# A decoder trunk of two layers: the seventh product moved between two halves of an up projection, and a weight sum made by an accumulating DMA

## The chip, the cores and the metric

The kernel runs on one NeuronCore of a Trainium2 chip. The metric is the device time of one execution in microseconds; the time before is the median of three runs. TensorE does the matmuls, VectorE (DVE), ScalarE (ACT) and GpSimd (POOL) the elementwise work, SyncE (SP) issues most of the loads from HBM. Each engine takes its own instructions in a fixed order, and an instruction that waits for a semaphore holds up all that stand behind it on its engine.

## The reference

Two post-norm layers over 512 positions of width 1024, in float32. The first has retention and stick-breaking attention heads, the second differential attention; both end in the same gated MLP, and the change lies in that MLP alone:

```
def conv_ffn(x, w_up, conv_w, conv_b, w_down):
    S = x.shape[1]
    h = x @ w_up                                   # 512 x 5632
    hp = jnp.pad(h, ((0, 0), (CONV_W - 1, 0), (0, 0)))
    h = sum(hp[:, j:j + S] * conv_w[j] for j in range(CONV_W)) + conv_b
    u, g = jnp.split(h, 2, axis=-1)                # 2 x 2816
    return (jax.nn.silu(g) * u) @ w_down           # 2816 x 1024
...
for l in range(DEPTH):
    m = mixer(x)                                   # even or odd
    x = layer_norm(ALPHA * x + m, ln1_g[l], ln1_b[l])
    f = conv_ffn(x, w_up[l], conv_w[l], conv_b[l], w_down[l])
    x = layer_norm(ALPHA * x + f, ln2_g[l], ln2_b[l])
```

## The kernel before

**Precision.** Every large product is made of three matmuls (`mm3`, L148 to L150): each operand is split into a high part (ScalarE casts it, L132: `wh`) and a low part (VectorE subtracts, L134: `wl`), and high by high, high by low and low by high are added in PSUM.

**The MLP's stages.** The 2816 columns are 22 blocks of 128. `period(i)` (L535) does block i: `up_mm` makes its two halves, first the column block of u, then that of the gate, each 24 matmuls into a PSUM bank of its own (`mmps`). `conv_half` (L445) takes a half out of PSUM: one ScalarE activation (L447) and two VectorE instructions (L449). `gated` (L454) applies silu (ScalarE, L456) and multiplies (VectorE, L457).

**The down projection by groups.** Blocks 0 to 15 form four groups of four, and the down projection of a group is done as a 2 by 2 block product with seven products m1 to m7 in place of eight. The four periods of the next group issue them (j = 0 to 3 is the period's place in its group): after the up projection m2 and m1 at j = 0, m5 at j = 1, m6 and m3 at j = 2, m7 at j = 3, and m4 of the group at j = 0 of the group after. Each product is twelve matmuls, six into each of two PSUM banks. m1, m6, m7 and m4 share the pair `wine`, m2, m5 and m3 the pair `winc`. After each product VectorE adds or subtracts the two banks into the residual `x` (`update`, L478; its instruction is L485 at the first touch of a piece of x and L482 later). A product that writes a pair again waits until VectorE has read it: m4 waits for the update after m7, and the next m1, which starts the pair anew, for the update after m4.

**The weights.** w_down of a group is stored as four blocks 21, 11, 22, 12 of 1024 columns. Three sums of blocks are made in the tile `chain`: SyncE loads 11, and GpSimd's queue adds 12, then 22, then 21 by accumulating DMAs (L476); between them the two splits read the sum. The other products read two tiles `raw` of 2048 columns (`wsrc`, L184): half 0 holds blocks 21 and 11, half 1 blocks 22 and 12. In half 1 GpSimd adds block 22 onto block 12 (L192), which is the fourth sum. `raw` has two buffers, the split weights `wh`, `wl` three. Half 1 is loaded, added and split in the `begin_to` of period j = 1 (L545).

**The order.** In the periods the order of ScalarE, VectorE and GpSimd is the order of the code, as is TensorE's everywhere. At j = 0 with g >= 1 the code issues: both up halves; `conv_half` of the first; the pending low parts of the group (`left`); the split of `chain` and the chain's next DMA; `conv_half` of the second and `gated`; then m4 of the group before with its update, m2 and m1 with theirs, and the split of the weights of block i + 2. Two layers with four groups each make eight m4 (three of the four groups of a layer have one in front of their m2 and m1; the fourth m4 stands in block 20).

Of the kernel before, what the change touches and what calls it, by code (L numbers as in the profile page):

```python
# [13 lines left out]
ALU = mybir.AluOpType  # L14
# [5 lines left out]
S = 512  # L20
# [6 lines left out]
ALPHA = (2 * DEPTH) ** 0.25  # L27
# [6 lines left out]
UNIT = 1024  # L34
# [80 lines left out]
class Build:  # L115
# [64 lines left out]
    def prefetch(self, ahead):  # L180
        while self.csrc and sum(c.n for c in self.cget.values()) < ahead * UNIT:
            self.begin()

    def wsrc(self, key):  # L184
        nc = self.nc
        if key[0] == "quad":
            _, l, g, half = key
            raw = self.load(self.a["w_quad"][l][g][:, half * 2 * UNIT:(half + 1) * 2 * UNIT])
            c = self.weights(self.wp)
            if half:  # L190
                self.split(raw, c, 0)
                nc.gpsimd.tensor_tensor(raw[:, UNIT:], raw[:, UNIT:], raw[:, :UNIT], op=ALU.add)  # L192
                return self.split(raw, c, UNIT)
            return self.split(raw, c, 0, UNIT)
        if key[0] == "tail":
            _, l, i = key
            raw = self.load(self.a["w_down"][l][i])
            return Pair(*(self.split(raw[:, a:a + UNIT], self.weights(self.w2, UNIT), 0) for a in (0, UNIT)))
        src = self.a[key[0]]
        for i in key[1:]:  # L200
            src = src[i]
        raw = self.load(src)
        return self.split(raw, self.weights(self.wp), 0, UNIT)
# [155 lines left out]
    def setup(self, ctx):  # L359
        nc = self.nc  # L360
        P_ = lambda name, bufs=1, **kw: ctx.enter_context(self.pool(name, bufs, **kw))
        self.ctx = ctx
        self.constp = P_("const")
        self.smallp = P_("small", 3)
        self.xtp = P_("xt")
        self.rawp = P_("raw", 2)
        self.wp = P_("w", 3)
        self.actp = P_("act", 16)
        self.mmps1 = P_("mmps", 3, space=PSUM)
        self.trps = P_("trps", 2, space=PSUM)  # L370
        self.dramp = P_("dram", 1, space=DRAM)
        self.mmi = 0
        self.mmpools = [(self.mmps1, "mm")]
        self.x = P_("xn", 1, side="right").tile([P, TB, DM], F32, tag="x", name="x")
        self.new_xT()
        self.ident = self.constp.tile([P, P], F32, tag="ident", name="ident")
        make_identity(nc, self.ident)
        self.mhalf = self.constp.tile([P, 8], F32, tag="mhalf", name="mhalf")
        nc.vector.memset(self.mhalf, -0.5)
        self.one = self.constp.tile([P, 1], F32, tag="one", name="one")  # L380
        nc.vector.memset(self.one, 1.0)
# [15 lines left out]
    def ffn(self, l, ln1):  # L397
        nc = self.nc
        with ExitStack() as c2:
# [44 lines left out]
            def conv_half(i, f, ps):  # L444
                tag, n = ("cu", 3) if f == i else ("cg", 2)  # L445
                t = tp.tile([P, S], F32, tag=tag, name=self.nm("cvt"), bufs=n)
                nc.scalar.activation(t, ps, AF.Identity, bias=cv[:, f, 3:4], scale=cv[:, f, 2:3])  # L447
                for d, c in ((1, 1), (2, 0)):
                    nc.vector.scalar_tensor_tensor(  # L449
                        out=t[:, d:], in0=ps[:, :S - d], scalar=cv[:, f, c:c + 1], in1=t[:, d:],  # L450
                        op0=ALU.mult, op1=ALU.add)
                return t
# [12 lines left out]
            full = slice(0, S)  # L465
            banks, quads, touched = {}, {}, set()

            def chain(g, *blocks):

                for b in blocks:  # L470
                    src = self.a["w_quad"][l][g][:, BLOCKS.index(b) * UNIT:(BLOCKS.index(b) + 1) * UNIT]
                    if b == "11":
                        self.chain = self.chainp.tile([P, UNIT], F32, tag="chain", name=self.nm("chain"))
                        nc.sync.dma_start(out=self.chain, in_=src)
                    else:
                        nc.gpsimd.dma_start(out=self.chain, in_=src, accum_op=ALU.add)  # L476

            def update(ps, tb, half, sign):  # L478
                xs = self.x[:, tb, half * S:(half + 1) * S]
                op = ALU.add if sign > 0 else ALU.subtract  # L480
                if (tb, half) in touched:
                    nc.vector.tensor_tensor(xs, xs, ps, op=op)  # L482
                else:
                    touched.add((tb, half))
                    nc.vector.scalar_tensor_tensor(out=xs, in0=xs, scalar=ALPHA, in1=ps, op0=ALU.mult, op1=op)  # L485

            def product(g, name):

                if name in ("m5", "m6", "m4"):
                    w = quads.pop((g, {"m5": "p1", "m6": "p2", "m4": "p4"}[name]))  # L490
                    at = 0
                else:
                    if name in ("m2", "m3"):
                        quads[g, name] = self.chunk(("quad", l, g, int(name == "m3")), 0)
                    w = quads[g, "m2" if name in ("m2", "m1") else "m3"]
                    at = UNIT if name in ("m1", "m7") else 0
                for tau in range(2):
                    if name == "m1":
                        banks["e", tau] = ps2.tile([P, S], F32, tag="e", name=self.nm("wine"), bufs=2)
                    elif name in ("m2", "m5"):  # L500
                        banks["c", tau] = self.trps.tile([P, S], F32, tag="tr", name=self.nm("winc"))
                    ps = banks["e" if name in ("m1", "m6", "m7", "m4") else "c", tau]
                    first = name in ("m1", "m2", "m5")
                    ts = slice(tau * P, (tau + 1) * P)
                    for kk in range(2):
                        h, l_ = ops[g, name, kk]
                        self.mm3(ps, h[:, ts], l_[:, ts], *w.get(at + kk * S, S), first and kk == 0, kk == 1,
                                 skip_group_check=not first)
                    lo, hi = tau, 2 + tau
                    tb, half, sign = {"m1": (lo, 0, -1), "m2": (lo, 0, 1), "m5": (hi, 1, 1), "m6": (lo, 1, 1),  # L510
                                      "m3": (lo, 1, 1), "m7": (hi, 1, 1), "m4": (hi, 0, -1)}[name]
                    update(ps, tb, half, sign)

            keys = []
            for i in range(NPAIR):
                keys.append(("w_up", l, i))
                g, j = i // 4 - 1, i % 4
# [5 lines left out]
            w = [self.chunk(("w_up", l, i), 4) for i in range(2)]  # L523
            pss = [[self.mmps() for _ in range(2)] for _ in range(2)]
# [10 lines left out]
            def period(i, left):  # L535
                g, j = i // 4 - 1, i % 4
                quad = 0 <= g < QUADS
                w = self.chunk(("w_up", l, i), 0)
                pss = [self.mmps(), self.mmps()]
                for k in range(2):  # L540
                    self.up_mm(w, k, pss[k], full)
                if not quad:
                    self.begin_to(("w_up", l, i + 2) if i + 2 < NPAIR else dk[2 * (i + 2 - NPAIR)])
                elif j < 3:
                    self.begin_to((("w_up", l, i + 1), ("quad", l, g, 1), ("w_up", l, i + 1))[j])  # L545
                u = conv_half(i, i, pss[0])
                if left:
                    left()
                if quad and j < 3:
                    name = ("p1", "p2", "p4")[j]  # L550
                    quads[g, name] = self.split(self.chain, self.weights(self.w2, UNIT), 0)
                    if j < 2:
                        chain(g, ("22", "21")[j])
                if j == 2 and g + 1 < QUADS:
                    chain(g + 1, "11", "12")
                left = gated(i, u, conv_half(i, NPAIR + i, pss[1]))
                if j == 0 and g >= 1:
                    product(g - 1, "m4")
                if quad:
                    for name in (("m2", "m1"), ("m5",), ("m6", "m3"), ("m7",))[j]:  # L560
                        product(g, name)
                    if j in (0, 2):
                        self.begin_to(("w_up", l, i + 2))
                return left

            E = mybir.EngineType
# [17 lines left out]
            for u in range(8):  # L584
                tb, half = u // 2, u % 2
                if u < 2:
                    ps = first[u]
                    down_mm(ps, 0, half, LASTN - 1)
                else:
                    ps = self.mmps()  # L590
# [587 lines left out]
```

## Time and profile before

| | |
|---|---|
| median of 3 runs | 1245.32 us (1243.57 to 1248.01) |
| profiled execution | 1244.74 us, of which the span is 1242.9 us |
| TensorE's granted clock, mean | 0.993 of full speed |
| busy share of the span | TensorE 97%, VectorE 70%, ScalarE 47%, GpSimd 15% |
| DMA | 140.13 MB, mean 113 GB/s |
| GpSimd's add of block 22 (L192) | 8 times, 2383 to 2677 ns, median 2401 ns |

The span runs from the first instruction to the last. Rows of the timeline give the start in us, the duration in us, engine, line, operation and tiles (out<-in), and in brackets how long the engine was idle before it and what ended that. "x2" is two instructions in a row, with the duration of both together. A matmul row shows 0.39 us because matmuls overlap in the pipeline; their starts are 0.23 us apart at full clock.

### The profile page before, as it was taken

How to read it: one execution, taken by the hardware profiler on the slowest of the kernel's cores; microseconds unless marked ns; L12 is line 12 of the kernel's file. 1: busy time of each engine (PE TensorE's matmuls, PEld its weight loads, DVE VectorE, ACT ScalarE, POOL GpSimd, SP SyncE). 2: the span in 40 equal slices, each digit the busy share in tenths (PEclk: the TensorE clock that was granted, in tenths of full speed). 3: DMA queues.
4: the chain of work that ended last, by engine and by line, in shares of the span. 5: the costliest groups of instructions: out<-in, count | busy, mean ns of one | idle time of the engine just before them, and what ended most of it. 6: DMA issues, size and time to landing. Idle time of an engine off the chain costs nothing.

```text
span 1242.9 us, 15110 instructions
## 1 busy us (share of the span) xinstructions
PE 1208.8 (97%) x5876; PEld 1001.4 (81%) x5876; DVE 869.6 (70%) x1324; ACT 581.2 (47%) x902; POOL 180.3 (15%) x238
## 2 busy tenths in 40 slices
PE   8999999999999999999999999999999999998997
PEld 6888877888887888788878888787988878787886
DVE  4866588776778677766655658776678777766664
ACT  5455565444534443433335658763444444443331
POOL 0211132211212121200000101011022211211000
PEclk9999999999999999999999999999999999998999
DMA  8322112333363535332252213223435444435111
GB/s 317 125 85 87 50 70 75 104 127 113 87 185 92 165 99 157 114 119 102 105 166 102 77 51 111 86 70 112 136 102 152 122 134 126 121 116 144 68 68 68
DMA packets 28175, 140.13 MB, mean 113 GB/s; under 512 B 3830, under 2 KB 4639, under 8 KB 15560
## 3 DMA queue, kind: packets, MB, share of 16 engines
q1 hardware_dynamic: 24648, 126.59, 28.7%
q0 software_dynamic: 3456, 12.58, 6.6%
q8 instruction: 46, 0.75, 0.3%
q14 instruction: 25, 0.20, 0.1%
HBM read 137.04 MB, written 4.74 MB: 114 GB/s over the span
## 4 chain that ended last, share of the span: by engine, by line
PE 79%; DVE 11%; ACT 5%; issue 2%; POOL 1%; DMA 1%; POOLq 0%; DVEq 0%; ACTq 0%; SPq 0%
PE mmps L148 21%; PE mmps L149 21%; PE mmps L150 21%; DVE wl L134 3%; PE wine L148 2%; PE wine L150 2%; PE wine L149 2%; DVE cvt L449 1%; PE winc L149 1%; PE winc L148 1%; PE winc L150 1%; PE dacc L939 1%; DVE cvt L457 1%; DVE actl L346 1%; PE dz L338 1%
## 5 line engine op out<-in xcount | busy, mean ns | idle before, releaser
L148 PE MATMUL mmps<-xTh,wh 128*128 128x512 f32 (+1 forms) x1008 | 384.8, 382 | 5.7 <-ACT wh L230 5.2
L149 PE MATMUL mmps<-xTl,wh 128*128 128x512 f32 (+1 forms) x1008 | 380.4, 377 | 0.9 <-DVE xTl L1080 0.9
L150 PE MATMUL mmps<-xTh,wl 128*128 128x512 f32 (+1 forms) x1008 | 379.8, 377 | 0.5 <-DVE wl L134 0.5
L134 DVE TENSOR_TENSOR wl<-raw,wh 128x1024 fp32r<-128x1024 f32 x196 | 240.1, 1265 | 33.0 <-ACT wh L132 32.7
L132 ACT CAST wh<-raw 128x1024 fp32r<-128x1024 f32 x196 | 195.3, 1045 | 76.9 <-PE mmps L149 35.8
L148 PEld LDWEIGHTS mmps<-xTh,wh 128*128 128x128 f32 x1008 | 190.6, 189 | 39.8 <-ACT wh L230 5.2
L150 PEld LDWEIGHTS mmps<-xTh,wl 128*128 128x128 f32 x1008 | 190.4, 189 | 36.1 <-DVE wl L134 1.0
L149 PEld LDWEIGHTS mmps<-xTl,wh 128*128 128x128 f32 x1008 | 190.6, 189 | 34.2 <-DVE xTl L1080 1.6
L449 DVE SCALAR_TENSOR_TENSOR cvt<-mmps,cv,cvt 128x511 f32<-128x511 f32 (+1 forms) x176 | 130.7, 747 | 109.1 <-ACT cvt L447 106.2
L447 ACT ACTIVATE cvt<-mmps,cv 128x512 f32<-128x512 f32 x88 | 68.3, 778 | 215.3 <-PE mmps L150 215.3
L148 PE MATMUL mmps<-wh,acth 128*128 128x512 f32 x224 | 91.4, 408 | 0.1
L150 PE MATMUL mmps<-wh,actl 128*128 128x512 f32 x224 | 88.5, 395 | 0.0
L149 PE MATMUL mmps<-wl,acth 128*128 128x512 f32 x224 | 88.3, 394 | 0.0
L148 PE MATMUL mmps<-wh,xTh 128*128 128x512 f32 x160 | 64.9, 406 | 0.0
L456 ACT ACTIVATE cvt<-cvt 128x512 f32<-128x512 f32 x44 | 27.8, 632 | 77.5 <-DVE cvt L449 77.5
L457 DVE TENSOR_TENSOR cvt<-cvt,cvt 128x512 f32<-128x512 f32 x44 | 39.4, 895 | 33.4 <-ACT cvt L456 33.4
L150 PE MATMUL mmps<-wh,xTl 128*128 128x512 f32 x160 | 62.6, 391 | 0.0
L149 PE MATMUL mmps<-wl,xTh 128*128 128x512 f32 x160 | 62.5, 390 | 0.0
L476 POOL DMA_DIRECT2D chain<-in_w_quad x24 | 21.4, 890 | 235.8 <-DVE wl L134 161.9
L150 PEld LDWEIGHTS mmps<-wh,actl 128*128 128x128 f32 x224 | 42.4, 189 | 10.3 <-DVE actl L349 0.5
L148 PEld LDWEIGHTS mmps<-wh,acth 128*128 128x128 f32 x224 | 42.4, 189 | 9.7 <-DVE x L276 0.7
L149 PEld LDWEIGHTS mmps<-wl,acth 128*128 128x128 f32 x224 | 42.4, 189 | 7.8
(190 smaller groups left out, 1800.1 us busy)
## 6 DMA issues: line engine op xcount, KB each, us to landing
raw<-in_w_up SPq DMA_DIRECT2D x44, 1024.0 KB, 5.0
raw<-in_w_quad SPq DMA_DIRECT2D x16, 1024.0 KB, 4.9
chain<-in_w_quad POOLq DMA_DIRECT2D x24, 512.0 KB, 6.1
raw<-in_w_ot SPq DMA_DIRECT2D x8, 1024.0 KB, 4.8
raw<-in_w_et SPq DMA_DIRECT2D x6, 1024.0 KB, 4.8
raw<-in_w_en SPq DMA_DIRECT2D x6, 1024.0 KB, 4.9
raw<-in_w_down SPq DMA_DIRECT2D x6, 1024.0 KB, 5.0
raw<-in_w_oe SPq DMA_DIRECT2D x4, 1024.0 KB, 4.8
```

Of the source, the lines that this page charges most:

```text
L132: nc.scalar.copy(c.h[:, sl], raw[:, sl])
L134: nc.vector.tensor_tensor(c.l[:, sl], raw[:, sl], c.h[:, sl].bitcast(F32), op=ALU.subtract)
L148: mm(out, lh, rh, start=start, stop=False, **kw)
L149: mm(out, lh, rl, start=False, stop=False, **kw)
L150: mm(out, ll, rh, start=False, stop=stop, **kw)
L338: self.nc.tensor.matmul(out, lhs, B[:, 2 + m, 0:n], start=False, stop=True)
L346: nc.vector.tensor_tensor(l, src, h.bitcast(F32), op=ALU.subtract)
L447: nc.scalar.activation(t, ps, AF.Identity, bias=cv[:, f, 3:4], scale=cv[:, f, 2:3])
L449: nc.vector.scalar_tensor_tensor(out=t[:, d:], in0=ps[:, :S - d], scalar=cv[:, f, c:c + 1], in1=t[:, d:], op0=ALU.mult, op1=ALU.add)
L456: nc.scalar.activation(g, g, AF.Silu)
L457: nc.vector.tensor_tensor(u, u, g, op=ALU.mult)
L476: nc.gpsimd.dma_start(out=self.chain, in_=src, accum_op=ALU.add)
```

## The change

`product` no longer issues its own update but returns what `update` needs. In the period at j = 0 with g >= 1, m4 of the group before is issued between the two up halves, and its update after `conv_half` of the first half. And half 1 of a group's weights is loaded by `load_quad` at the end of period j = 0; block 22 is added onto block 12 there by a DMA from GpSimd's queue that reads block 22 from HBM again. The split of half 1 stays at j = 1, and casts both parts before both subtractions.

```diff
+    def load_quad(self, key):
+
+        _, l, g, half = key
+        src = self.a["w_quad"][l][g][:, half * 2 * UNIT:(half + 1) * 2 * UNIT]
+        raw = self.load(src)
+        if half:
+            self.nc.gpsimd.dma_start(out=raw[:, UNIT:], in_=src[:, :UNIT], accum_op=ALU.add)
+            self.early[key] = raw
+        return raw
+
     def wsrc(self, key):
         nc = self.nc
         if key[0] == "quad":
-            _, l, g, half = key
-            raw = self.load(self.a["w_quad"][l][g][:, half * 2 * UNIT:(half + 1) * 2 * UNIT])
-            c = self.weights(self.wp)
-            if half:
-                self.split(raw, c, 0)
-                nc.gpsimd.tensor_tensor(raw[:, UNIT:], raw[:, UNIT:], raw[:, :UNIT], op=ALU.add)
-                return self.split(raw, c, UNIT)
-            return self.split(raw, c, 0, UNIT)
+            raw = self.early.pop(key, None) or self.load_quad(key)
+            return self.split(raw, self.weights(self.wp), 0, UNIT)
...
-                for k in range(2):
-                    self.up_mm(w, k, pss[k], full)
+                self.up_mm(w, 0, pss[0], full)
+                m4 = j == 0 and g >= 1 and product(g - 1, "m4")
+                self.up_mm(w, 1, pss[1], full)
...
                 u = conv_half(i, i, pss[0])
+                if m4:
+                    update(m4)
                 if left:
                     left()
...
                 left = gated(i, u, conv_half(i, NPAIR + i, pss[1]))
-                if j == 0 and g >= 1:
-                    product(g - 1, "m4")
                 if quad:
                     for name in (("m2", "m1"), ("m5",), ("m6", "m3"), ("m7",))[j]:
-                        product(g, name)
+                        update(product(g, name))
                     if j in (0, 2):
                         self.begin_to(("w_up", l, i + 2))
+                    if j == 0:
+                        self.load_quad(("quad", l, g, 1))
                 return left
```

TensorE in the first layer's second group, before, at the end of the first up half (`mmps_3119` is the bank of the first half, `mmps_3120` that of the second, `wine_2784` the first bank of m4):

```order
L148 MATMUL mmps_3119<-xTh_2062,wh_3025 128x512
L149 MATMUL mmps_3119<-xTl_2063,wh_3025 128x512
L150 MATMUL mmps_3119<-xTh_2062,wl_3026 128x512
L148 MATMUL mmps_3120<-xTh_2062,wh_3025 128x512
L149 MATMUL mmps_3120<-xTl_2063,wh_3025 128x512
```

The same place after the change:

```order
L148 MATMUL mmps_3119<-xTh_2062,wh_3025 128x512
L149 MATMUL mmps_3119<-xTl_2063,wh_3025 128x512
L150 MATMUL mmps_3119<-xTh_2062,wl_3026 128x512
L148 MATMUL wine_2784<-wh_2982,a_357_2521 128x512
L149 MATMUL wine_2784<-wl_2983,a_357_2521 128x512
```

m4's twelve matmuls stand now in front of the 24 of the second half; before they stood behind them.

VectorE in the same period, before (`wine_2784`, `wine_2792` are m4's banks, `winc` those of m2, `wine_3238` the first of m1):

```order
L449 SCALAR_TENSOR_TENSOR cvt_3185<-mmps_3119,cv_2232,cvt_3185 128x510
L346 TENSOR_TENSOR actl_3190<-q_3091,acth_3189 128x512
L346 TENSOR_TENSOR actl_3194<-q_3091,acth_3193 128x512
L134 TENSOR_TENSOR wl_3198<-chain_2986,wh_3197 128x1024
L449 SCALAR_TENSOR_TENSOR cvt_3202<-mmps_3120,cv_2232,cvt_3202 128x511
L449 SCALAR_TENSOR_TENSOR cvt_3202<-mmps_3120,cv_2232,cvt_3202 128x510
L457 TENSOR_TENSOR cvt_3185<-cvt_3185,cvt_3202 128x512
L485 SCALAR_TENSOR_TENSOR x<-x,wine_2784 128x512
L485 SCALAR_TENSOR_TENSOR x<-x,wine_2792 128x512
L482 TENSOR_TENSOR x<-x,winc_3222 128x512
L482 TENSOR_TENSOR x<-x,winc_3230 128x512
L482 TENSOR_TENSOR x<-x,wine_3238 128x512
```

And after the change (its lines are numbered 4 or 5 higher here):

```order
L454 SCALAR_TENSOR_TENSOR cvt_3197<-mmps_3119,cv_2232,cvt_3197 128x510
L490 SCALAR_TENSOR_TENSOR x<-x,wine_2784 128x512
L490 SCALAR_TENSOR_TENSOR x<-x,wine_2791 128x512
L350 TENSOR_TENSOR actl_3204<-q_3091,acth_3203 128x512
L350 TENSOR_TENSOR actl_3208<-q_3091,acth_3207 128x512
L134 TENSOR_TENSOR wl_3212<-chain_2986,wh_3211 128x1024
L454 SCALAR_TENSOR_TENSOR cvt_3216<-mmps_3120,cv_2232,cvt_3216 128x511
L454 SCALAR_TENSOR_TENSOR cvt_3216<-mmps_3120,cv_2232,cvt_3216 128x510
L462 TENSOR_TENSOR cvt_3197<-cvt_3197,cvt_3216 128x512
L487 TENSOR_TENSOR x<-x,winc_3222 128x512
L487 TENSOR_TENSOR x<-x,winc_3229 128x512
L487 TENSOR_TENSOR x<-x,wine_3238 128x512
```

The update after m4 has moved up by six instructions; it no longer stands behind the second half's convolution and the multiplication. On GpSimd the accumulating DMA stands in the very place of the add: behind the chain's DMA of block 22, in front of that of block 21. SyncE's loads keep their order, but for one load for the second layer's mixer at the end of the first layer, which now stands behind two small ones.

## Rows read from the trace of the kernel before

**Rows 1.** the page: span; TensorE's busy us, share, instructions
```profile
span 1242.9 us, 15110 instructions
PE 1208.8 (97%) x5876; PEld 1001.4 (81%) x5876; DVE 869.6 (70%) x1324; ACT 581.2 (47%) x902; POOL 180.3 (15%) x238
```

**Rows 2.** TensorE's waits on wine banks: us in all, times, longest
```profile
PE wine L148 <- DVE x L482: 7.6, 3, 3.2
PE wine L148 <- DVE x L485: 3.2, 2, 1.7
```

**Rows 3.** timeline of TensorE: first matmuls of m2 and m4 (start, us)
```profile
328.42 0.39 PE L148 MATMUL winc<-wh,ah 128*128 128x512 f32 x1
388.51 0.39 PE L148 MATMUL wine<-wh,a 128*128 128x512 f32 x1
391.31 0.40 PE L148 MATMUL winc<-wh,ah 128*128 128x512 f32 x1
453.28 0.39 PE L148 MATMUL wine<-wh,a 128*128 128x512 f32 x1
516.55 0.39 PE L148 MATMUL wine<-wh,a 128*128 128x512 f32 x1
584.16 0.39 PE L148 MATMUL wine<-wh,a 128*128 128x512 f32 x1
989.40 0.39 PE L148 MATMUL wine<-wh,a 128*128 128x512 f32 x1
1119.04 0.39 PE L148 MATMUL wine<-wh,a 128*128 128x512 f32 x1
1188.24 0.39 PE L148 MATMUL wine<-wh,a 128*128 128x512 f32 x1
```

**Rows 4.** windows behind two waits: busy by engine, PEclk, DMA share, GB/s
```profile
525.00:530.00 5.00, 4.85 (x14) 3.88 (x15) 3.03 (x6) 0.55 (x1) 0.00 (x0) 0.66 0.00 0
1128.00:1134.00 6.00, 6.00 (x14) 4.72 (x15) 2.84 (x5) 0.93 (x2) 0.00 (x0) 0.50 0.01 3
```

**Rows 5.** timeline at the first wait: VectorE, GpSimd, TensorE
```profile
386.84 1.52 DVE L449 SCALAR_TENSOR_TENSOR cvt<-mmps,cv,cvt 128x511 f32<-128x511 f32 x2
392.15 2.39 POOL L192 TENSOR_TENSOR raw<-raw 128x1024 f32<-128x1024 f32 x1 [0.27 <-DMA raw<-in_w_quad]
392.90 2.20 DVE L457 TENSOR_TENSOR cvt<-cvt,cvt 128x512 f32<-128x512 f32 x1 [0.76 <-ACT cvt L456]
395.02 1.27 DVE L485 SCALAR_TENSOR_TENSOR x<-x,wine 128x512 f32<-128x512 f32 x2
395.84 0.47 PE L148 MATMUL wine<-wh,ah 128*128 128x512 f32 x1 [1.57 <-DVE x L485]
```

**Rows 6.** timeline, earlier there: update after m7, second up half
```profile
378.22 0.69 DVE L457 TENSOR_TENSOR cvt<-cvt,cvt 128x512 f32<-128x512 f32 x1 [0.76 <-ACT cvt L456]
380.93 1.27 DVE L482 TENSOR_TENSOR x<-x,wine 128x512 f32<-128x512 f32 x2
383.07 0.39 PE L148 MATMUL mmps<-xTh,wh 128*128 128x512 f32 x1
```

**Rows 7.** timeline there: SyncE's load, GpSimd's chain DMA, ScalarE's casts
```profile
386.95 0.33 SPq L143 DMA_DIRECT2D raw<-in_w_quad  x1
391.00 0.88 POOL L476 DMA_DIRECT2D chain<-in_w_quad  x1 [8.57 <-DVE wl L134]
398.88 2.01 ACT L132 CAST wh<-raw 128x1024 fp32r<-128x1024 f32 x2 [4.12 <-PE wine L150]
```

**Rows 8.** GpSimd's chain DMAs: landing; page part 3, their queue
```profile
DMA to landing us min/median/max: 5.7/6.1/7.7
q0 software_dynamic: 3456, 12.58, 6.6%
```

**Rows 9.** timeline, next periods: second sum's low part, and m6
```profile
406.58 1.22 DVE L134 TENSOR_TENSOR wl<-chain,wh 128x1024 fp32r<-128x1024 f32 x1
423.26 0.39 PE L148 MATMUL wine<-wh,acth 128*128 128x512 f32 x1
```

More of the change, by code (lines that the diff above doesn't have):

```diff
@@ L372, in setup @@
         self.mmi = 0
+        self.early = {}
         self.mmpools = [(self.mmps1, "mm")]
@@ L476, in chain, with update @@
                         nc.gpsimd.dma_start(out=self.chain, in_=src, accum_op=ALU.add)
[L478 to L485, printed above, removed]
+            def update(parts):
+                for ps, tb, half, op in parts:
+                    xs = self.x[:, tb, half * S:(half + 1) * S]
+                    if (tb, half) in touched:
+                        nc.vector.tensor_tensor(xs, xs, ps, op=op)
+                    else:
+                        touched.add((tb, half))
+                        nc.vector.scalar_tensor_tensor(out=xs, in0=xs, scalar=ALPHA, in1=ps, op0=ALU.mult, op1=op)
             def product(g, name):
+                res = []
                 if name in ("m5", "m6", "m4"):
@@ L509, in product @@
                     lo, hi = tau, 2 + tau
-                    tb, half, sign = {"m1": (lo, 0, -1), "m2": (lo, 0, 1), "m5": (hi, 1, 1), "m6": (lo, 1, 1),
-                                      "m3": (lo, 1, 1), "m7": (hi, 1, 1), "m4": (hi, 0, -1)}[name]
-                    update(ps, tb, half, sign)
+                    tb, half = {"m1": (lo, 0), "m2": (lo, 0), "m5": (hi, 1), "m6": (lo, 1), "m3": (lo, 1),
+                                "m7": (hi, 1), "m4": (hi, 0)}[name]
+                    res.append((ps, tb, half, ALU.subtract if name in ("m1", "m4") else ALU.add))
+                return res
             keys = []
```

## The prediction

> **What bounds the kernel now.** I read the page first. TensorE is busy for 1208.8 of the span's 1242.9 us [rows 1]; VectorE comes next with 70%. Nothing but TensorE's own idle or slow time is to be had, some 34 us of idle in all. So the second view was the list of TensorE's waits. In the MLP two entries stand out, both on the first product that needs the `wine` banks anew, both ended by VectorE's update: three waits with 7.6 us together and two with 3.2 us [rows 2]. That is m1, waiting for the update after m4: five waits, 10.8 us.
>
> The third view, TensorE's timeline, tells what those waits cost in all. From one group's m4 to the next TensorE's program is always the same (four up projections, seven products), so the distance should be constant. In the first group, which has no m4 in front of its m2, the distance from m2 to the next m2, with one m4 in it, is 391.31 - 328.42 = 62.89 us [rows 3]. The six groups that have m4 in front of m1 take 64.77, 63.27 and 67.61 us in the first layer, and 129.64 (two together) and 69.20 us in the second [rows 3], 394.49 us in all. Five of them hold the five waits; the sixth, 63.27, holds none that the list counts and bounds the undisturbed pitch from above. I take 63.0, nearer to the group that surely waits for nothing: 394.49 - 6 x 63.0 = 16.5 us are lost. With 62.89 it is 17.2, with 63.27 it is 14.9.
>
> The 16.5 us can be checked from other rows. 10.8 us are the waits. Behind the two longest waits the granted clock falls: 0.66 over 5 us and 0.50 over 6 us [rows 4], where 1.00 is 2.4 GHz and 0.50 is 1.2 GHz. That is 5 x 0.34 + 6 x 0.50 = 4.7 us. The remaining 1.0 us is the refilling of the matmul pipeline after each wait (a first matmul of 0.47 us in rows 5 against 0.39).
>
> Why is VectorE late there? In rows 5 it takes the first up half at 386.84. Then come other work, the second half, and the multiplication at 392.90, which takes 2.20 us where the same instruction takes 0.69 at 378.22 [rows 6]; it lies beside GpSimd's add of 2.39 us, which started at 392.15. Only at 395.02 does the update after m4 start, and TensorE's m1 at 395.84.
>
> **Part 1: m4 between the two halves.** The matmuls are the same. A half lasts 388.51 - 383.07 = 5.44 us, a product 391.31 - 388.51 = 2.80 us [rows 3, 6]. So in this group m4 now starts at 383.07 and ends at 385.87, the second half ends at 391.31, m2 begins there as before, and m1 could begin at 391.31 + 2.80 = 394.11; it began at 395.84, a delay of 1.73 us.
>
> m4's update now stands behind the first half's convolution on VectorE, which ends at 386.84 + 1.52 = 388.36 [rows 5]. Two instructions of 1.27 us together end at 389.63, 4.5 us ahead of m1. The wait goes, and nothing on VectorE is late in its place: what moves behind the update (1.27 us) used to stand before it, and the second half itself now ends 2.80 us later, so its convolution waits for TensorE in any case.
>
> What is late next? m4 itself: it starts one half earlier, and needs the update after m7. That runs at 380.93 for 1.27 us, so both banks are free at 382.20, 0.87 us before 383.07; the first bank, which m4 needs first, about 0.6 us earlier [rows 6]. The margin is thin but positive, and nothing in the change stands in front of that update.
>
> The second half's path (convolution, silu, product, split) comes 2.80 us later. Its next user on TensorE is a whole up projection away or further: 10.88 us (two halves) in block 20, more in the groups. Cost: 0. If that cover were gone it would cost up to 2.80 us in each of eight places.
>
> **Part 2: the fourth sum by DMA.** Eight adds of 2.4 us leave GpSimd, which is idle for 85% of the span. The VectorE instruction beside each gets back up to 2.20 - 0.69 = 1.5 us. On the path this is worth nothing beyond part 1, since the update no longer stands behind it; without part 1 it would shorten most of the waits. Added are eight DMAs of 512 KB (4.2 MB on 140) and a new wait: the second cast of half 1 on ScalarE waits for the landing.
>
> When does it land? The load of half 1 is issued at 386.95 and has landed by 392.15, where the add could start [rows 5, 7]. The chain's DMA stands ahead on GpSimd at 391.00 and moves back by the update's 1.27 us to 392.27; with its 0.88 us the new DMA is issued at 393.15. No row has an accumulating DMA onto `raw`, or two from GpSimd's queue back to back. Lower bound: it lands like the chain's, 6.1 us after issue, at 399.3. Upper bound: the two are served one after the other; the 24 DMAs of that queue took 6.6% of 1242.9 us [rows 8], 3.4 us each, so the second lands 3.4 us behind the first (392.27 + 6.1 = 398.4), at 401.8. I take 401.8, as the two are issued 0.9 us apart.
>
> Who waits? ScalarE wants the first cast at 398.88 - 1.73 = 397.15 and the second 1.0 us later, at 398.15 [rows 7]. It waits 1.1 to 3.6 us. Behind it on ScalarE and VectorE stand the convolution of the next period's first half, which TensorE finishes at 396.91 + 5.44 = 402.35, and the second weight sum's split. That split's low part was ready at 407.80, and m6, its first user, starts at 423.26: 15.5 us of slack [rows 9], against a delay of at most about 1 us. Cost: 0. Below nothing it cannot go, as no TensorE wait hangs on half 1 now.
>
> A rule of the Trainium skill speaks against this edit (SBUF — State Buffer, section "SBUF: two separate sides"): a DMA from GpSimd's queue can starve while VectorE holds the port through which its descriptors are written, in its example 620 ns became about 3100. Here the 24 such DMAs landed in 5.7 to 7.7 us with VectorE busy for 70% of the time [rows 1, 8], so no starving of that size shows; by the rule the landing would be an estimated 2.5 us later (from that page's two figures), still far from m6, and the sum would stay.
>
> **The sum.** Profiled execution 1244.74 us (span 1242.9, 1.84 around it) - 16.5 = 1228.2. The median of the runs is 0.6 us above the profiled execution, so 1228.8 us. With the pitch's bounds: 1228.1 to 1230.4.
>
> **The rivals.**
>
> *The clock is not given back.* If the two half-clock stretches are not the doing of the waits, 4.7 us stay: 1233.5. For it: rows 4 show the stretches, not their cause. Against: both lie where m1 begins in the two groups with the largest distances, 8 to 9 us behind their m4 [rows 3, 4].
>
> *m4 waits in m1's stead.* If the update after m7 slips by more than 0.87 us against TensorE, each further us costs one us in eight places. VectorE's largest slip in rows 5 is 1.5 us, beside the add that goes; at twice that, 3.0 us, the cost is 8 x 2.1 = 17 us at worst and all of the gain: 1246. A slip of 1.5 us costs 8 x 0.6 = 5: 1234. Against: the work ahead of that update is untouched.
>
> *The move does not do what it says.* m1 has other needs (its weights' low part, the operands); if one of these is due at the same moment, the wait only changes its name: 1245. Against: the weights' subtraction stands ahead of the 386.84 row on VectorE, over 7 us before m1.
>
> *The DMA lands too late: slower.* ScalarE stands still on the second cast, with all convolutions behind it. It reaches TensorE only beyond the 15.5 us of rows 9, a landing at 398.15 + 15.5 = 413.7, 20.5 us after issue. To be slower by 0.3% (3.7 us, about what a measurement of this kernel tells from no change) it must take 16.5 + 3.7 = 20.2 us in eight places, 2.5 each: 23 us from issue to landing against 7.7 at most in rows 8. Then the time is 1249 or more.
>
> **How the numbers follow.** Forecast 0.81; clock not given back 0.05; m4 waits 0.07 (two thirds of it at a small slip); wait renamed 0.04; landing too late 0.03. Faster by over 0.3%: 0.81 + 0.05 + 0.05 = 0.91; within: 0.04 + 0.01 = 0.05; slower: 0.03 + 0.01 = 0.04. The range goes from 1228.1 less the spread of the runs (1245.32 - 1243.57 = 1.75), 1226, up to the small-slip and clock cases (1234) with the same spread, 1236.
>
> **What would show it.** Right: TensorE's list has no wait on `wine` for VectorE; the distances from m4 to m4 are all 63.0 to 63.3 us; the clock is 1.00 behind every m1; the multiplication after the gate takes 0.7 us at j = 0; ScalarE shows some us of waiting for a DMA into `raw` at j = 1, and TensorE none after it. Wrong: a wait of m4 for the update after m7, in every group alike; a TensorE wait on an up half or on m6 at j = 1 or 2; or distances that stay above 64 us without a wait.

## The result

| | before | changed |
|---|---|---|
| median of the runs, us | 1244.44 (4 runs, 1242.00 to 1248.01) | 1226.70 (4 runs, 1226.15 to 1226.91) |
| profiled execution, us | 1244.74 | 1226.91 |
| its span, us | 1242.9 | 1225.1 |

The ratio is 0.9854, with a 95% interval of 0.9829 to 0.988: the change makes the kernel faster by 17.7 us. The forecast was 1228.8.

The page of the changed kernel (span; busy us, share of the span and instructions by engine; GpSimd's DMA queue with packets, MB and share), against [rows 1, 8]:

```profile
span 1225.1 us, 15125 instructions
PE 1202.3 (98%) x5876; PEld 998.8 (82%) x5876; DVE 859.0 (70%) x1324; ACT 581.1 (47%) x902; POOL 167.8 (14%) x238
q0 software_dynamic: 4608, 16.78, 8.5%
```

TensorE executes the same 5876 instructions. VectorE and GpSimd lose some 11 and 13 us of busy time, and the queue carries eight more transfers. The list of TensorE's waits (us in all, times, longest) holds no entry on `wine` any more, where [rows 2] had five waits with 10.8 us. Its longest entries now are:

```profile
PE mmps L148 <- ACT wh L234: 4.5, 1, 4.5
PE atr L710 <- ACT zp L702: 3.6, 2, 2.1
PE dz L341 <- ACT kB L333: 1.3, 2, 1.1
```

The timeline of TensorE, first matmuls of m4 in both layers (start and duration in us), against the m4 rows of [rows 3]:

```profile
382.56 0.39 PE L148 MATMUL wine<-wh,a 128*128 128x512 f32 x1
445.48 0.39 PE L148 MATMUL wine<-wh,a 128*128 128x512 f32 x1
508.39 0.39 PE L148 MATMUL wine<-wh,a 128*128 128x512 f32 x1
571.30 0.39 PE L148 MATMUL wine<-wh,a 128*128 128x512 f32 x1
976.29 0.39 PE L148 MATMUL wine<-wh,a 128*128 128x512 f32 x1
1039.20 0.39 PE L148 MATMUL wine<-wh,a 128*128 128x512 f32 x1
1102.12 0.39 PE L148 MATMUL wine<-wh,a 128*128 128x512 f32 x1
1165.03 0.39 PE L148 MATMUL wine<-wh,a 128*128 128x512 f32 x1
```

The distances from m4 to m4 are 62.91 or 62.92 us everywhere: (571.30 - 382.56) + (1165.03 - 976.29) = 377.48 us for the six groups that took 394.49 before. So 17.0 of the 17.8 us of span come from them. The rest lies outside: the first m2 starts at 327.91 us in place of 328.42 [rows 3], and from the fourth m4 to the fifth, between the layers, it takes 404.99 us in place of 405.24.

VectorE and TensorE of the changed kernel at the first m1 that has an m4 in front of it (start, duration; in brackets idle time before and its releaser), against [rows 5, 6]:

```profile
380.43 1.27 DVE L487 TENSOR_TENSOR x<-x,wine 128x512 f32<-128x512 f32 x2
386.33 1.52 DVE L454 SCALAR_TENSOR_TENSOR cvt<-mmps,cv,cvt 128x511 f32<-128x511 f32 x2
387.77 1.27 DVE L490 SCALAR_TENSOR_TENSOR x<-x,wine 128x512 f32<-128x512 f32 x2
391.83 1.53 DVE L454 SCALAR_TENSOR_TENSOR cvt<-mmps,cv,cvt 128x511 f32<-128x511 f32 x2 [0.45 <-ACT cvt L452]
393.57 0.39 PE L148 MATMUL wine<-wh,ah 128*128 128x512 f32 x1
394.13 0.69 DVE L462 TENSOR_TENSOR cvt<-cvt,cvt 128x512 f32<-128x512 f32 x1 [0.76 <-ACT cvt L461]
```

The update after m4 (387.77) ends at 389.04, 4.5 us ahead of m1 at 393.57, which waits for nothing. The multiplication takes 0.69 us in place of 2.20. The update after m7 ends at 381.70, 0.86 us ahead of m4 at 382.56.

Windows around two m1 of the changed kernel, at the places of [rows 4] (us; busy us of TensorE, its weight loads, VectorE, ScalarE and GpSimd, each with its instructions; granted clock, DMA share, GB/s):

```profile
517.00:524.00 7.00, 7.00 (x33) 5.74 (x32) 5.07 (x9) 4.58 (x6) 1.78 (x2) 1.00 0.70 117
1110.00:1120.00 10.00, 10.00 (x46) 8.24 (x45) 8.07 (x11) 5.27 (x7) 1.77 (x2) 1.00 0.66 120
```

The granted clock is 1.00 in both, where it was 0.66 and 0.50; windows of 8 us at the four other m1 behind an m4 (from 393, 456, 986 and 1049 us) read 1.00 too. Last, the new transfers and who waits for them, in three views: GpSimd's issues (ns, starts) and their landing; ScalarE's waits for them (us in all, times, longest); and ScalarE's timeline at the first:

```profile
L190 POOL DMA_DIRECT2D raw<-in_w_quad x8: 1037/1104/1189, 332.2 to 1112.0; - x8
DMA to landing us min/median/max: 7.6/8.2/9.3
```
```profile
ACT wh L132 <- DMA raw<-in_w_quad: 26.6, 8, 4.7
```
```profile
400.54 1.05 ACT L132 CAST wh<-raw 128x1024 fp32r<-128x1024 f32 x1 [2.97 <-DMA raw<-in_w_quad]
```

ScalarE stands still for 3.3 us on average in eight places (26.6 / 8), and no wait of TensorE follows from it.

### The profile page after: what moved, and what is told of

It reads as the page before. It is cut to its first block, busy times and chain, and to the rows that moved or that the text cites. A ratio compares the mean times of both kernels' runs of the same rounds, so it can differ in the third digit from the quotient of the medians.

```text
span 1225.1 us, 15125 instructions
## 1 busy us (share of the span) xinstructions
PE 1202.3 (98%) x5876; PEld 998.8 (82%) x5876; DVE 859.0 (70%) x1324; ACT 581.1 (47%) x902; POOL 167.8 (14%) x238
## 4 chain that ended last, share of the span: by engine, by line
PE 88%; DVE 5%; ACT 4%; POOL 1%; DMA 1%; issue 1%; POOLq 0%; DVEq 0%; ACTq 0%
PE mmps L148 22%; PE mmps L149 22%; PE mmps L150 22%; PE wine L149 2%; PE wine L148 2%; PE wine L150 2%; PE winc L149 2%; PE winc L148 2%; PE winc L150 2%; PE dacc L949 1%; DVE wl L134 1%; PE dz L342 1%; DVE t L698 1%; PE dz L341 1%; POOL zp L701 1%
## 5 line engine op out<-in xcount | busy, mean ns | idle before, releaser
L462 DVE TENSOR_TENSOR cvt<-cvt,cvt 128x512 f32<-128x512 f32 x44 | 30.4, 692 | 32.6 <-ACT cvt L461 32.6
L1063 ACT ACTIVATE junk<-x,lst 128x1024 bf16<-128x1024 f32 x16 | 18.4, 1150 | 64.5 <-DVE lst L1060 64.4
```

What stands on the lines that cost most here:

```text
L462: nc.vector.tensor_tensor(u, u, g, op=ALU.mult)
L1063: nc.scalar.activation(junk, x, AF.Square, bias=st[:, 0:1], accum_out=st[:, 1:2])
```

## The experiments

The theory: TensorE lost its time because m4's update stood behind the second half's multiplication in VectorE's order; the update's place is what counts, GpSimd's add made it worse, and the DMA is hidden behind slack. The rivals: the matmuls' place counts; the DMA brings part of the gain, or costs something; and m4 or half 1 could still become the late ones. Edits are against the changed kernel; the kernel before ran beside each group (medians 1243.12, 1244.71 and 1244.12).

**The move alone.** GpSimd's add is back, and half 1 is loaded, added and split at j = 1 again.

```diff
 wsrc:
-    raw = self.early.pop(key, None) or self.load_quad(key)
-    return self.split(raw, self.weights(self.wp), 0, UNIT)
+    _, l, g, half = key
+    raw = self.load(self.a["w_quad"][l][g][:, half * 2 * UNIT:(half + 1) * 2 * UNIT])
+    c = self.weights(self.wp)
+    if half:
+        self.split(raw, c, 0)
+        nc.gpsimd.tensor_tensor(raw[:, UNIT:], raw[:, UNIT:], raw[:, :UNIT], op=ALU.add)
+        return self.split(raw, c, UNIT)
+    return self.split(raw, c, 0, UNIT)
...
 period:
-    if j == 0:
-        self.load_quad(("quad", l, g, 1))
```

> m4 and its update stand as in the changed kernel; the fourth weight sum is made by GpSimd's add again, as before. Theory A (the update's place on VectorE carries the whole gain; the DMA has nothing left to save): 1226 to 1228 us, m4 to m4 distances 62.9 us, no TensorE wait on wine; the multiplication beside the add takes about 2.2 us again, and nobody waits for it. Theory B (the add's drag on VectorE is a part of the loss in its own right): 1231 us or more, with TensorE waits on wine of 0.5 us and up.

Measured: 1226.34 us (ratio 0.987, 0.9855 to 0.9885), distances of 62.91 and 62.92, no wait on `wine`. GpSimd and VectorE in its timeline:

```profile
392.29 2.70 POOL L202 TENSOR_TENSOR raw<-raw 128x1024 f32<-128x1024 f32 x1
394.12 1.43 DVE L468 TENSOR_TENSOR cvt<-cvt,cvt 128x512 f32<-128x512 f32 x1 [0.76 <-ACT cvt L467]
```

The add still slows the multiplication (1.43 us against 0.69, and not the 2.2 that were expected), and it costs nothing: once the update has moved, no one waits there. The DMA half of the change brings nothing on top.

**The DMA alone.** m4 and its update are where they were.

```diff
-m4 = j == 0 and g >= 1 and product(g - 1, "m4")
...
-if m4:
-    update(m4)
...
 left = gated(i, u, conv_half(i, NPAIR + i, pss[1]))
+if j == 0 and g >= 1:
+    update(product(g - 1, "m4"))
```

> The sum by the accumulating DMA, m4 and its update behind both up halves as before. Theory A: the multiplication takes 0.7 us in place of 2.2, so the update comes 1.5 us earlier; the waits of m1 shrink to about 0.2 us in four groups and 1.5 to 1.7 us in the last group of each layer, where a split stands ahead of the update as well, and the clock does not fall behind waits of that size; some 4.7 us of the 17 remain: 1231 us (1229 to 1234). Theory B (the DMA does nothing for TensorE): 1243 to 1246 us.

Measured: 1231.98 us (0.9916, 0.9901 to 0.9931). TensorE's waits on `wine`:

```profile
PE wine L148 <- DVE x L487: 2.9, 2, 1.5
```

Four of six distances are 63.27 or 63.28, two 64.66 and 64.67, which is 382.44 us in all. So either half takes away most of the loss, by the distances 12 us this one (394.49 - 382.44) and 17 the other: two cures for one wait.

**Matmuls early, update late.**

```diff
-if m4:
-    update(m4)
...
 left = gated(i, u, conv_half(i, NPAIR + i, pss[1]))
+if m4:
+    update(m4)
```

> The changed kernel, with m4's matmuls between the halves, but its update behind the gate's multiplication, where it stood before. Theory A (what counts is where VectorE reads m4's banks): the second half now ends 2.8 us later and the update behind it comes at about 395.3 where m1 wants 394.1, so m1 waits about 2.0 us in four groups and 3.4 us in the last group of each layer, with the clock falling there: 1243 to 1248 us, nothing gained. Theory C (what counts is that the matmuls are early): 1232 us or less.

Measured: 1243.56 us (1.0011, 0.999 to 1.0032, ten runs): the whole gain is gone, with the DMA still in place. TensorE's waits on `wine`:

```profile
PE wine L148 <- DVE x L487: 10.1, 4, 3.2
PE wine L148 <- DVE x L490: 3.7, 2, 1.8
```

From the DMA alone (1231.98 us) this kernel differs only in the place of m4's matmuls, and it is 11.6 us slower. So early matmuls do harm where the update stands late: they put the second half 2.80 us later, and with it the update behind it.

**Matmuls late, update early.** m4 is issued behind both halves, its update just ahead of the second half's convolution.

```diff
 self.up_mm(w, 0, pss[0], full)
-m4 = j == 0 and g >= 1 and product(g - 1, "m4")
 self.up_mm(w, 1, pss[1], full)
+m4 = j == 0 and g >= 1 and product(g - 1, "m4")
...
-if m4:
-    update(m4)
...
+if m4:
+    update(m4)
 left = gated(i, u, conv_half(i, NPAIR + i, pss[1]))
```

> The changed kernel, with m4's matmuls behind both halves as before, and its update on VectorE just ahead of the second half's convolution. Theory A: m4 ends at about 391.4, the update runs 391.5 to 392.8, m1 wants the first bank at 394.1 and does not wait: 1226.5 to 1229 us, distances 62.9 to 63.1 us. Theory C (the matmuls must be early): 1235 us or more, with waits on wine of over 1 us.

Measured: 1226.98 us (0.9875, 0.9861 to 0.989), distances of 63.02, no wait on `wine`. With the run before it, this settles what counts: the matmuls at their old place and the update moved give all of the gain, the reverse gives none. Both have the DMA; the update moved alone beside GpSimd's add was not run.

**Two and five more instructions ahead of the update after m7.** They test the margin of m4, the next to be late.

```diff
-update(product(g, name))
+parts = product(g, name)
+for k in range(2 if name == "m7" else 0):   # 5 in the second
+    xs = self.x[:, k % TB, 0:S]
+    nc.vector.scalar_tensor_tensor(out=xs, in0=xs, scalar=0.0, in1=xs, op0=ALU.mult, op1=ALU.add)
+update(parts)
```

> The changed kernel with two harmless VectorE instructions (x*0+x on 128x512, 0.67 us each) ahead of the update after m7, in each of the eight places. The margin of m4's first bank read from the profiles is 1.46 us, that of the second bank 2.3 us; 1.34 us of slip stay inside it: no TensorE wait on wine, 1226 to 1228 us. If the margin were only the 0.87 us between the end of the whole update and the end of the first half, m4 would wait 0.5 us in eight places: 1230 to 1232 us.

> The same with five such instructions, 3.35 us of slip. Theory (m4's new place is safe only by its margin): m4 waits about 2.0 us in three groups of a layer and about 1.2 us in the last, where the margin is larger, 14.4 us in all: 1240 to 1246 us, nearly all of the gain gone, with TensorE waits on wine for VectorE in front of m4. Rival (the slip is taken up elsewhere): 1226 to 1230 us.

Measured with two: 1231.88 us (0.9907, 0.9884 to 0.993), a miss. VectorE and GpSimd in its timeline, and from the list of waits TensorE's on `wine`:

```profile
378.68 0.92 POOL L424 TENSOR_TENSOR q<-cvt,q 128x256 f32<-128x256 f32 x1
379.68 1.07 POOL L425 TENSOR_TENSOR q<-cvt,q 128x256 f32<-128x256 f32 x1
378.92 2.38 DVE L572 SCALAR_TENSOR_TENSOR x<-x 128x512 f32<-128x512 f32 x2
381.22 1.27 DVE L487 TENSOR_TENSOR x<-x,wine 128x512 f32<-128x512 f32 x2
```
```profile
PE wine L148 <- DVE x L487: 4.4, 6, 0.7
```

The two took 2.38 us and not 1.34; they lie beside GpSimd's subtractions (L424 and L425). So the update slipped by 2.30 us. m4 waited up to 0.74 us in six places. That makes the margin 2.30 - 0.74 = 1.56 us, near the 0.87 + 0.6 of the prediction's first bank.

Measured with five: 1249.93 us (1.0042, 1.0026 to 1.0058), slower than before and above the 1240 to 1246 that were expected. The update slips by 4.11 us, not 3.35, the wait should be 4.11 - 1.56 = 2.55, and it is 2.54 (the list of waits, and TensorE's timeline at the first):

```profile
PE wine L148 <- DVE x L487: 16.7, 8, 2.5
```
```profile
385.12 0.63 PE L148 MATMUL wine<-wh,a 128*128 128x512 f32 x1 [2.54 <-DVE x L487]
```

Windows of 7 us behind its six waits of 2.53 or 2.54 us (columns as above):

```profile
385.00:392.00 7.00, 6.88 (x23) 5.55 (x24) 6.96 (x9) 0.45 (x1) 0.00 (x0) 0.76 0.42 146
452.00:459.00 7.00, 6.62 (x22) 5.33 (x23) 6.96 (x9) 0.72 (x1) 0.00 (x0) 0.76 0.43 138
520.00:527.00 7.00, 7.00 (x32) 5.74 (x31) 6.96 (x9) 0.00 (x0) 0.00 (x0) 1.00 0.48 173
991.00:998.00 7.00, 6.99 (x30) 5.75 (x31) 6.96 (x8) 0.35 (x1) 0.00 (x0) 1.00 0.47 157
1056.00:1063.00 7.00, 6.27 (x20) 5.00 (x21) 6.96 (x9) 1.06 (x2) 0.00 (x0) 0.76 0.35 114
1124.00:1131.00 7.00, 6.99 (x30) 5.75 (x31) 6.96 (x8) 0.35 (x1) 0.00 (x0) 1.00 0.45 158
```

From m4 to m4 a group takes 65.72 us where the clock held behind its first m4 (991.01 to 1056.73) and 67.26 to 67.28 where it fell, against 62.91. So a wait of 2.53 us costs 0.28 us beyond itself, and the lower clock another 1.55. 16.7 of waits, 8 x 0.28 = 2.2 beyond them and 3 x 1.55 = 4.7 of lower clock make 23.6, against the 23.2 us that this kernel takes over the changed one. This is the prediction's rival "m4 waits in m1's stead", with its cost.

**The DMA later.** Memsets of a scratch tile stand ahead of the accumulating DMA on GpSimd, 10, 28, 50 and 70 in four kernels.

```diff
+scr = self.chainp.tile([P, 256], F32, tag="scr", name=self.nm("scr"))
+for _ in range(10):   # 28, 50, 70
+    self.nc.gpsimd.memset(scr, 0.0)
 self.nc.gpsimd.dma_start(out=raw[:, UNIT:], in_=src[:, :UNIT], accum_op=ALU.add)
```

> The changed kernel with ten GpSimd memsets (128x256 on a scratch tile) ahead of the accumulating DMA, so that it lands some 5 to 9 us later. Theory (15.5 us of slack behind the second cast of half 1): ScalarE waits longer, TensorE not at all: 1226 to 1228 us. Rival (ScalarE's wait is passed on to TensorE by the convolutions behind it): 1227 plus eight times several us, 1250 or more.

> The same with 28 memsets: the DMA lands 14 to 25 us later than in the changed kernel, at 414 to 425 us on the first such place's clock, where the second cast is wanted at 397.6. Theory: TensorE is reached from a landing at about 413 on; each us beyond costs about one us in each of the eight groups: 1230 to 1320 us by the landing that the profile shows, with TensorE waits on m6 or on the up projection behind it. Rival (the slack is larger than read): 1226 to 1230 us even with a landing beyond 416.

> As with 28 memsets, with 50: one takes 0.37 us from start to start, so the DMA lands near 417.4 on the first such place's clock, 19.8 us after the second cast is wanted. Theory (slack of 15.5 us to m6): TensorE waits there for 4 us in each of eight groups, up to 1226 + 34 = 1260 us, above 1235 in any case. Rival (the order behind the cast leaves more slack than the row showed): 1226 to 1230 us.

> With 70 memsets the DMA lands near 424.8, 27.2 us after the cast is wanted. Theory: 11.7 us of waiting in each of eight groups, about 1320 us, the waits on m6 or on the up projection behind it. Rival (more slack than read): under 1280 us.

ScalarE's waits for the DMA, one row from each of the four kernels, in that order:

```profile
ACT wh L132 <- DMA raw<-in_w_quad: 41.5, 8, 6.6
```
```profile
ACT wh L132 <- DMA raw<-in_w_quad: 94.1, 8, 13.3
```
```profile
ACT wh L132 <- DMA raw<-in_w_quad: 163.0, 8, 21.2
```
```profile
ACT wh L132 <- DMA raw<-in_w_quad: 224.3, 8, 28.7
```

| memsets | ScalarE's mean wait, us | time, us (two runs each) | over the 1226.1 of 28 memsets | by 15.5 us of slack |
|---|---|---|---|---|
| 10 | 5.2 | 1225.78 | 0 | 0 |
| 28 | 11.8 | 1226.11 | 0 | 0 |
| 50 | 20.4 | 1275.5 | 49 | 8 x 4.9 = 39 |
| 70 | 28.0 | 1330.09 | 104 | 8 x 12.5 = 100 |

A memset took 0.37 us from start to start, less than the expectations took, so the DMA of the 28 had landed by 409.26 us at the first place with an m4, short of the 413 from which TensorE was to be reached; the 50 passed it. The 1275.5 lies above the 1260 that was expected at most. One place with 50 memsets and the same with 70 (ScalarE's cast at the landing, then m6, with the releasers of their waits):

```profile
425.05 1.05 ACT L132 CAST wh<-raw 128x1024 fp32r<-128x1024 f32 x1 [20.81 <-DMA raw<-in_w_quad]
429.98 0.50 PE L149 MATMUL wine<-wl,acth 128*128 128x512 f32 x1 [1.72 <-DVE wl L134]
```
```profile
440.35 1.04 ACT L132 CAST wh<-raw 128x1024 fp32r<-128x1024 f32 x1 [28.36 <-DMA raw<-in_w_quad]
443.06 0.79 PE L148 MATMUL wine<-wh,acth 128*128 128x512 f32 x1 [7.59 <-ACT wh L132]
445.29 0.80 PE L149 MATMUL wine<-wl,acth 128*128 128x512 f32 x1 [1.43 <-DVE wl L134]
```

m6 waits, as was said, but later than was said: ScalarE may stand still for 20.81 - 1.72 = 19.1 or 28.36 - 7.59 - 1.43 = 19.3 us there before TensorE does, and for 17.5 to 19.4 at all sixteen places of the two runs, not for 15.5. The 15.5 leave out that ScalarE in the kernel before stood idle behind its second cast anyway, until the next up half was there:

```profile
404.32 0.78 ACT L447 ACTIVATE cvt<-mmps,cv 128x512 f32<-128x512 f32 x1 [3.44 <-PE mmps L150]
```

15.5 + 3.4 = 18.9 us lies within what was measured. The last column comes near the times all the same because it also leaves out what stands behind m6's waits: TensorE's waits on `wine` and `winc` add up to 28.5 us of the 49 with 50 memsets and to 81.2 of the 104 with 70, while its mean granted clock falls from 0.997 to 0.984 and 0.963. Two errors of opposite sign met there.

In the changed kernel ScalarE waits 3.3 us on average and 4.7 at most; some 13 us of slack are left.

No run beats the changed kernel: 1225.78, 1226.34 and 1226.98 are within a microsecond of 1226.70, less than these measurements tell apart. The move alone does as well without the 4.2 MB of transfers.

## Why the prediction was right

- **The bound, and the price by distances.** Right. 394.49 us became 377.48. The undisturbed distance is 62.91, not the 63.0 that was taken; 62.89 had been the lower bound. That is 0.5 us of the 1.3 by which the profiled execution beats its forecast (1226.91 against 1228.2); the other 0.75 lies outside the groups and no term had it. Another 0.8 us of the 2.1 between the forecast and the median is the step from the profiled execution to the median, taken as 0.6 us upwards from three runs; of the changed kernel the median lies 0.2 below. So 1226.70 came near the lower end of the range, 1226.
- **What the 16.5 us were made of.** The 1.0 us left for refilling was somewhat small: a wait costs 0.28 us beyond itself in the run with five instructions, 1.4 for five. The 4.7 us of lower clock belong to the one profiled execution. Executions of that kernel lay between 1236.63 and 1248.78 us in one group of runs; that the profiled one, 1244.74, lay near the median was luck which the price by distances relied on.
- **Part 1.** Right, in its times too: m1 was to find its banks free for 4.5 us, and does; m4 was to have 0.87 us on its second bank, and has 0.86. The two runs that part the matmuls from the update show the cause, VectorE's order. The runs with a slip show that the margin that counts is the first bank's, 1.56 us. The price of the rival, taken from the second bank's 0.87, was too high for a small slip: the 5 us that it set for a slip of 1.5 us came at 2.30 (1231.88 against 1226.70).
- **Part 2.** Worth nothing beyond part 1, and most of the gain without it, as said: 1226.34 for the move alone, 1231.98 for the DMA alone. The landing came at 400.5 us, 8.2 us after issue, between the bounds of 399.3 and 401.8; ScalarE's wait of 2.97 lies in the 1.1 to 3.6. The value taken, the upper bound, was 1.3 us too late, which the slack hides. The slack itself was taken some 2 to 4 us too small, since ScalarE's own idle time ahead of the next convolution was left out.
- **The rivals.** The clock was given back (1.00 behind each of the six m1). The wait did not change its name. A late landing does decide once the slack is used up, but some 13 us beyond the longest of the present waits, and then it costs more than m6's waits alone.

The 0.5 us ahead of the groups need no cause in the change: kernels that share its program up to the first m2 start it anywhere from 326.40 to 327.94 us. That the two slow stretches of [rows 4] were the waits' doing rests on their going with them, and on the slow stretches behind the waits that were made again.

## What to carry to other kernels

Where a program repeats, take the distance between equal instructions: what it exceeds the undisturbed one by is the price of a wait, clock and refilling included, which a list of waits shows only in part. An instruction that frees a PSUM bank goes ahead of slow work in its engine's order. Where the matmuls stand did not matter here once that was so (1226.70 and 1226.98 us); while it was not, moving them forward cost 11.6 us. Then work out the margin of whatever is late next, since a slip of a few microseconds there takes the gain back.

## What was not expected of the hardware

**Equal waits, unequal clock.** In the run with five instructions, six waits of 2.53 or 2.54 us are followed by a granted clock of 0.76 over 7 us in three places and of 1.00 in the other three. The 0.76 is a mean: from 386 to 388 us the clock reads 0.50, which is 1.2 GHz, and from 389 us on 1.00, which is 2.4 GHz. With matmuls early and update late, two waits of 3.2 us show the same (columns as above):

```profile
526.00:530.00 4.00, 4.00 (x19) 3.28 (x18) 3.30 (x6) 1.39 (x3) 0.00 (x0) 1.00 0.27 52
1127.00:1132.00 5.00, 4.97 (x15) 3.96 (x16) 2.71 (x5) 0.81 (x2) 0.00 (x0) 0.66 0.31 60
```

That may be why the kernel before spreads over 12 us in one group of runs (1236.63 to 1248.78) and the changed one, without such waits, over 0.8. The mean granted clock goes the same way, 0.998 in the shortest of those runs and 0.991 in the longest, which over their spans is 2.5 and 11.2 us; what decides between equal places stays open.

**Two engines at one port.** A 128x512 multiplication of VectorE with two inputs from SBUF lasted until 0.56 us after the end of GpSimd's add beside it, twice: with the add of [rows 5] from 392.90 to 395.10, the add ending at 394.54; in the move alone from 394.12 to 395.55, the add ending at 394.99. So its 2.20 and 1.43 us are set by the rest of the add and are not a property of the multiplication. The Trainium skill (SBUF — State Buffer, section "Who interferes with whom") says that VectorE, reading two inputs from SBUF, contends with a GpSimd instruction that reads SBUF, and that the second to issue is blocked until the first is done; these two rows agree, and so do the two instructions of the run with a slip, which took 2.38 us and ended at 381.30, 0.55 us after the last of GpSimd's subtractions.

**A DMA right behind another.** The accumulating DMA lands 8.2 us after issue (median) where it is issued 0.6 us behind the chain's. With ten memsets between them the same view gives:

```profile
DMA to landing us min/median/max: 5.8/6.1/6.3
```

So 2.1 us of its landing go with the other being close in front. What makes them is not shown. If the two were simply served one after the other, a later issue would shorten the landing; with matmuls late and update early six of the eight were issued 1.5 to 1.9 us behind the chain's, and landed no sooner:

```profile
DMA to landing us min/median/max: 7.6/8.4/8.7
```
